# The beginning of a two-layer trunk: the first two k-tiles' scale and shift on TensorE, c loaded later, head pieces per k-tile

## The chip, the cores and the metric

The kernel runs on one core of a Trainium2 chip. The metric is device microseconds of one execution. A core has five engines that the profile names: PE (TensorE matmul, with its weight loads as PEld), DVE (VectorE), ACT (ScalarE), POOL (GpSimd) and SP (SyncE, which here issues every DMA). Each takes its instructions strictly in its own order and waits at an instruction until what that needs is there.

## The reference: what is computed

A token block `x` (256 x 2048) goes through two layers. Each layer takes `c` (1 x 2048), forms `mod = silu(c) @ w + b`, splits it into `shift`, `scale` and `gate`, and feeds the mixer with a modulated input:

```python
mod = jax.nn.silu(c) @ w + b
shift, scale, gate = jnp.split(mod, 3, axis=-1)
# every layer: x <- LayerNorm(alpha*x + (1+gate) * mixer(x*(1+scale)+shift))
```

Layer one's mixer projects `h = x*(1+scale)+shift` with `in_w` (2048 x 10304) into z, x, B, C and dt, convolves, scans and gates, and projects back. Layer two is a dilated attention. Only the first use of `mod` and the projection behind it concern the change: 2048 scales and 2048 shifts, each a dot product of length 2048, are needed before the projection can read `h`. The 2048 rows of `h` (the contraction) are 16 k-tiles of 128; k-tile kt needs its own 128 scales and 128 shifts and nothing of the other k-tiles.

## The kernel before, in words

**Columns.** For each k-tile a 1 MB "column" of `ada` (128 outputs on partitions, 2048 inputs along the free dimension) is loaded for the scale and one for the shift (`ada_load`, L242). DVE multiplies it by `cb_` (silu of c on all 128 partitions, loaded by `bcast` at L67 as 1 MB and passed through Silu at L68) and sums along the free dimension in one instruction (`ada_dot`, L251). `ada_bias` (L256) adds the bias, ACT forms `htmp = x*scale+shift` (L413) and its rounded copy `hhi` (L414), DVE the rest `hlo` (L415); both are slices of the tile that the profile calls `actT`. `h_step` (L397) does one column; two make a k-tile.

**Pieces.** Weights come in 512 KB pieces `raw` (`load_piece`, L91, six buffers). `split` (L96) makes two tiles of each: `whi` on ACT (L99) and `wlo = raw - whi` on DVE (L101), four buffers each. TensorE then multiplies hi by hi, hi by lo and lo by hi. A piece of type "cm" (B, C, x columns; `cm_piece`, L125 to L127) holds two k-tiles of 512 output columns and is 24 products of 256 columns; a "tm" piece (z; `tm_mults`, L173 to L175) is 12 products of 512 columns. Every piece is about the same PE time.

**Order of the beginning.** A list of rows (L424) fixes the order of the pieces by hand: `b4:0.` is piece 0 (k-tiles 0 and 1) of column group b4, the dot says that the partial sum is put away into SBUF by ACT (L488), and `h` is a piece of the first four column groups, alternately of `win[0]` and `win[4]`, which accumulate in PSUM through all 16 k-tiles. As k-tiles become ready one by one, TensorE works on groups that use only the ready ones. A loop (L491 on) fetches piece and column ahead, splits pieces i and i+1, multiplies piece i, and runs `h_step` so that about four columns go with seven pieces (L519). Before the loop four columns and four pieces are requested and k-tiles 0 and 1 finished. A scheduler then sets the final order on each engine; SP issues the DMAs in the order in which they are requested, with at most eight under way.

Of the kernel before, what the change touches and what calls it, by code (L numbers as in the profile page):

```python
# [18 lines left out]
P = 128  # L19
L = 256  # L20
# [29 lines left out]
def trunk(ctx, tc, xT, x, c, par, cst, bias, lnrow, ada, wdt, win, wxs, wout, wk, wv, wbin, wbout, out):  # L50
# [16 lines left out]
    bcast(cb_, c)  # L67
    S.activation(cb_, cb_, AF.Silu)  # L68
# [4 lines left out]

    cons.tile([P, 32], F32, name="pad")
# [215 lines left out]
    with ExitStack() as cA:  # L290
# [14 lines left out]
        with ExitStack() as cS:  # L305
# [4 lines left out]
            begun = {("z", 0): (win[6], 6, szt[0]), ("z", 1): (win[7], 4, szt[1]),  # L310
                     ("xs", 1): (win[5], 4, as_cm(y[0])), ("bc", 2): (win[1], 4, as_cm(y[1])),
                     ("z", 2): (win[8], 14, y[2]), ("bc", 4): (win[2], 12, as_cm(y[3])), ("z", 4): (win[10], 6, y[4]),
                     ("bc", 6): (win[3], 12, as_cm(y[5])), ("z", 6): (win[12], 10, y[6]), ("z", 5): (win[11], 8, y[7])}
# [39 lines left out]
            def product(kind, g, pre=None):  # L353

                if kind == "xs" and g > 1:
                    return xs_wide(g)

                src, k0, part = begun.get((kind, g), (None, 0, None))
                if src is None:
                    src = win[{"bc": g // 2, "xs": 4 + g, "z": 6 + g}[kind]]  # L360
                if kind == "z":
                    ps = tm_chunk(src, hh_, hl_, rate=R, k0=k0, pre=pre)
                    if g not in sz:
                        sz[g] = p0.tile([P, 2, 512], F32, name="sz")
                    for b in range(2):
                        if part is not None:
                            V.tensor_tensor(part[:, b, :], ps[b], part[:, b, :], op=ALU.add)
                        S.activation(sz[g][:, b, :], part[:, b, :] if part is not None else ps[b], AF.Silu)
                    return
                ps = cm_quad(src, hhi, hlo, rate=R, k0=k0)  # L370
                t = tiles(ps)
                if part is not None:
                    for w in range(2):
                        V.tensor_tensor(part[:, 2 * w:2 * w + 2, :], ps[w], part[:, 2 * w:2 * w + 2, :], op=ALU.add)
                    t = [part[:, n, :] for n in range(4)]
                if kind == "xs":
                    xs_conv(g, t)
                else:
                    bc_conv(g, t)

            with ExitStack() as c0:
# [4 lines left out]
                raws, xts, late = [], {}, []  # L386
# [10 lines left out]
                def h_step():  # L397
# [4 lines left out]
                    if kind == "scale" and kt % 2 == 0 and kt:  # L402
                        fetch_x(kt)
                    ada_dot(0, kind, kt, raw)
                    if kt > 1:
                        pin[0] = None
# [11 lines left out]
                h_step.i = 0  # L418
# [5 lines left out]
                for row in ("b4:0. b6:0. h z2:0. b2:0 x1:0 h", "b2:1. x1:1. z1:0 z1:1. z4:0 h h",  # L424
# [3 lines left out]
                    for w in row.split():  # L428
                        if w == two:
                            n = -2 if sum(o[0] == -2 for o in order) == sum(o[0] == -1 for o in order) else -1  # L430
                            order.append((n, sum(o[0] == n for o in order), False))
# [3 lines left out]
                source = {"dt": wdt, -2: win[0], -1: win[4], **{n: p[0] for n, p in zip(names, begun.values())}}  # L435
                pss = {-2: first[0], -1: first[1]}
# [7 lines left out]
                fetch()  # L444
                fetch()
                fetch_x(0)
                nc.sync.dma_start(adab_, par[:, :NB])
                V.tensor_scalar(adab[:, :, :, 1:3], adab[:, :, :, 1:3], 1.0, None, op0=ALU.add)
                fetch_piece()
                fetch_piece()  # L450
                fetch()
                fetch_piece()
                for _ in range(2):
                    for _ in range(2):
                        h_step()
                    while late:
                        pin[0] = late.pop()().ins
                    fetch_piece()
# [31 lines left out]
                begin, done, ended, halves = {}, set(), [], {}  # L490
                for i, (k, q, ends) in enumerate(order):  # L491
                    fetch_piece()
                    if i == 16:
                        nc.sync.dma_start(prm, par[:, NB:])
# [10 lines left out]
                    z = str(k)[0] == "z"  # L505
# [4 lines left out]
                    if z:  # L510
# [8 lines left out]
                    while h_step.i < min(len(cols), 4 + (i + 1) * 4 // 7):  # L519
                        h_step()  # L520
# [555 lines left out]
def _layout(x, c, ada_w, ada_b, ln_g, ln_b, a_in_w, a_conv_w, a_conv_b, a_dt_bias,  # L1076
# [29 lines left out]
    def mask(delta, win_, dil):  # L1106
# [6 lines left out]
    ada = ada_w.reshape(2, D, 3, KT, P).transpose(0, 2, 3, 4, 1)  # L1113
# [4 lines left out]
    win = _pieces(np.concatenate([bc, xs[:, :1024], z], 1))  # L1118
    return {
        "xT": x[0].T.reshape(KT, P, L).transpose(1, 0, 2), "x": x[0], "c": c, "par": par, "cst": cst, "bias": bias,  # L1120
        "lnrow": np.stack([ln_g[0], ln_b[0], ln_g[1], ln_b[1]]),
        "ada": ada, "wdt": _dt(dt), "win": win, "wxs": _pieces(xs[:, 1024:], 256, 4),
# [23 lines left out]
```

## Time and profile before

| what | value |
|---|---|
| median of 3 runs | 1253.88 us (1252.72 to 1255.48) |
| the profiled execution's own time | 1253.52 us |
| its span in the profile | 1251.7 us |
| mean granted TensorE clock in the span | 0.998 |
| PE busy, share of the span | 1218.4 us, 97% |
| DVE busy, ACT busy | 1031.0 us, 704.5 us |
| HBM read | 332.47 MB |

All times below count from the start of the span. Starts and durations in the timeline rows are microseconds; a bracket behind a row says how long its engine had stood idle and what ended that. The rows that the argument uses are shown with it.

### The profile page before, as it was taken

To read this page: it belongs to the slowest core of one execution; us is meant where nothing else is said; L and a number is where in the kernel's file an instruction comes from. 1 tells how busy PE (TensorE), PEld (TensorE's weight loads), DVE (VectorE), ACT (ScalarE), POOL (GpSimd) and SP (SyncE) were. 2 spreads that over 40 slices of the span, in tenths; PEclk is the share of its full clock that TensorE was granted. 3 is DMA by queue.
4 is the path that set the end of the run, shared out by engine and by line. 5 is a ranking of instruction groups with operands and counts; after the bars stand their busy time and mean duration, and the time that the engine had idled before them with its cause. 6 is when DMAs were issued, how large, how long until landed. Compare 5 with 4: busy or idle time off the path is not lost.

```text
span 1251.7 us, 18740 instructions
## 1 busy us (share of the span) xinstructions
PE 1218.4 (97%) x7086; PEld 1043.1 (83%) x7086; DVE 1031.0 (82%) x1454; ACT 704.5 (56%) x1045; POOL 0.2 (0%) x4
## 2 busy tenths in 40 slices
PE   4999999999999999999999999999999999999997
PEld 4889998898888878788888788888878888888886
DVE  6999986999987988899778678879888866758777
ACT  3655477869588788754444544434445644445631
POOL 0000000000000000000000000000000000000000
PEclk9999999999999999999999999999999999999999
DMA  9999977687657556699998569989998774464641
GB/s 381 422 421 423 420 253 257 207 286 285 203 179 219 170 155 198 220 321 342 354 313 305 183 199 377 364 318 348 359 381 317 242 241 142 126 207 122 228 176 67
DMA packets 80586, 335.88 MB, mean 268 GB/s; under 512 B 9104, under 2 KB 9328, under 8 KB 67696
## 3 DMA queue, kind: packets, MB, share of 16 engines
q1 hardware_dynamic: 80496, 334.69, 74.7%
q8 instruction: 55, 0.90, 0.3%
q14 instruction: 35, 0.29, 0.1%
HBM read 332.47 MB, written 2.18 MB: 267 GB/s over the span
## 4 chain that ended last, share of the span: by engine, by line
PE 86%; DVE 6%; DMA 5%; issue 1%; ACT 1%; SPq 0%; DVEq 0%; ACTq 0%
PE acc L149 20%; PE acc L174 12%; PE acc L175 12%; PE acc L173 12%; PE acc L152 10%; PE acc L125 4%; PE acc L127 3%; PE acc L126 3%; DMA raw<-in_wk 3%; DMA araw<-in_ada 2%; DVE araw L251 1%; DVE wlo L101 1%; PE py L625 1%; DMA raw<-in_wv 1%; PE acc L809 1%
## 5 line engine op out<-in xcount | busy, mean ns | idle before, releaser
L99 ACT ACTIVATE whi<-raw 128x1024 fp32r<-128x1024 f32 x392 | 412.3, 1058 | 383.1 <-PE acc L175 142.1
L101 DVE TENSOR_TENSOR wlo<-raw,whi 128x1024 fp32r<-128x1024 f32 x392 | 473.5, 1222 | 141.0 <-ACT whi L99 137.0
L149 PE MATMUL acc<-actT,whi 128*128 128x512 f32 x1280 | 406.3, 398 | 0.0
L152 PEld LDWEIGHTS acc<-actT,wlo 128*128 128x128 f32 x1280 | 239.7, 188 | 62.2 <-DVE wlo L101 7.2
L174 PE MATMUL acc<-wlo,actT 128*128 128x512 f32 x688 | 269.9, 392 | 0.6 <-DVE wlo L101 0.5
L173 PE MATMUL acc<-whi,actT 128*128 128x512 f32 x688 | 266.6, 394 | 1.2 <-ACT actT L681 1.2
L152 PE MATMUL acc<-actT,wlo 128*128 128x256 f32 x1280 | 254.1, 280 | 3.9 <-DVE wlo L101 3.8
L251 DVE SCALAR_TENSOR_TENSOR araw<-araw,cb__72 128x2048 f32<-128x2048 f32 x96 | 219.4, 2285 | 8.9 <-DMA araw<-in_ada 8.6
L149 PEld LDWEIGHTS acc<-actT,whi 128*128 128x128 f32 x1280 | 196.5, 189 | 0.4
L175 PE MATMUL acc<-whi,actT 128*128 128x512 f32 x432 | 168.8, 391 | 0.0
L174 PEld LDWEIGHTS acc<-wlo,actT 128*128 128x128 f32 x688 | 129.3, 188 | 28.5 <-DVE wlo L101 2.8
L173 PEld LDWEIGHTS acc<-whi,actT 128*128 128x128 f32 x688 | 128.8, 188 | 27.2 <-ACT actT L681 1.7
L125 PE MATMUL acc<-actT,whi 128*128 128x256 f32 x384 | 109.0, 288 | 17.5 <-ACT actT L414 17.3
L126 PE MATMUL acc<-actT,whi 128*128 128x256 f32 x384 | 108.8, 286 | 0.0
L127 PE MATMUL acc<-actT,wlo 128*128 128x256 f32 x384 | 106.7, 286 | 1.9 <-DVE wlo L101 1.9
L175 PE MATMUL acc<-whi,ylo 128*128 128x512 f32 x256 | 100.7, 394 | 0.0
L175 PEld LDWEIGHTS acc<-whi,actT 128*128 128x128 f32 x432 | 81.1, 188 | 16.7
L125 PEld LDWEIGHTS acc<-actT,whi 128*128 128x128 f32 x384 | 74.3, 194 | 18.9 <-ACT actT L414 17.5
L127 PEld LDWEIGHTS acc<-actT,wlo 128*128 128x128 f32 x384 | 73.4, 195 | 2.2 <-DVE wlo L101 2.1
L126 PEld LDWEIGHTS acc<-actT,whi 128*128 128x128 f32 x384 | 74.7, 194 | 0.3
L175 PEld LDWEIGHTS acc<-whi,ylo 128*128 128x128 f32 x256 | 48.1, 188 | 9.7
L583 ACT ACTIVATE seg<-cbc,cumT 128x128 f32<-128x128 f32 x128 | 41.2, 390 | 5.6 <-PE py L625 4.9
(262 smaller groups left out, 1054.3 us busy)
## 6 DMA issues: line engine op xcount, KB each, us to landing
araw<-in_ada SPq DMA_DIRECT2D x96, 1024.0 KB, 7.7
raw<-in_win SPq DMA_DIRECT2D x112, 512.0 KB, 6.5
raw<-in_wout SPq DMA_DIRECT2D x64, 512.0 KB, 5.7
raw<-in_wbin SPq DMA_DIRECT2D x64, 512.0 KB, 4.1
raw<-in_wxs SPq DMA_DIRECT2D x48, 512.0 KB, 4.6
raw<-in_wv SPq DMA_DIRECT2D x48, 512.0 KB, 6.0
raw<-in_wk SPq DMA_DIRECT2D x48, 512.0 KB, 8.3
cbc<-cumd SPq DMA_DIRECT2D x16, 512.0 KB, 4.8
```

Of the source, the lines that this page charges most:

```text
L99: copied.append(S.activation(hi, raw, AF.Copy))
L101: latest.append(V.tensor_tensor(lo, raw, hi.bitcast(F32), op=ALU.subtract))
L125: T.matmul(o, hi[:, k, c_], ahi[:, kt, :], start=first, stop=False, skip_group_check=True)
L126: T.matmul(o, hi[:, k, c_], alo[:, kt, :], start=False, stop=False, skip_group_check=True)
L127: T.matmul(o, lo[:, k, c_], ahi[:, kt, :], start=False, stop=kt == k1 - 1, skip_group_check=True)
L149: T.matmul(ps[n], hi[:, k, n * P:n * P + P], both(kt), start=kt == 0, stop=False, skip_group_check=True)
L152: T.matmul(ps[n][:, 0, :], lo[:, k, n * P:n * P + P], high(kt), start=False, stop=kt == KT - 1, skip_group_check=True)
L173: T.matmul(o, h_, hi[:, k, :], start=kt == k0, stop=False, skip_group_check=part)
L174: T.matmul(o, h_, lo[:, k, :], start=False, stop=False, skip_group_check=part)
L175: end = T.matmul(o, l_, hi[:, k, :], start=False, stop=kt == k1 - 1, skip_group_check=part)
L251: V.scalar_tensor_tensor(raw, raw, 1.0, cb_, op0=ALU.mult, op1=ALU.mult, accum_out=mod[layer][:, ct, j:j + 1])
L583: S.activation(seg[:, hh, b, :], cbc[:, hh, b, :], AF.Relu, bias=cumT[:, b, h0 + hh:h0 + hh + 1], scale=-1.0)
```

## The change

k-tiles 0 and 1 no longer use columns, `cb_` or DVE's dot. Their weights are stored by input row: four 512 KB pieces per k-tile, each 128 inputs by (four input blocks of 128 scale/shift outputs). For each piece `ada_partial` runs four small products on TensorE: a stationary `ctile` of 32 columns of which only the first holds silu(c), and 256 moving columns, each product into its own 32 partitions of one PSUM tile. Sixteen products sum a k-tile; `ada_sum` copies that tile to SBUF on ACT, two products with ones add the 128 partitions up, DVE adds the bias, and ACT and DVE form `hhi` and `hlo` directly from x. silu(c) for this comes from a new small input `cT` (128 x 16). `cb_` is loaded in two halves behind the first pieces, and its Silu is done after k-tile 1. Twelve products of a 128 x 128 tile of ones stand at the head of TensorE's queue ("warm").

The head groups (`h`) become one piece per k-tile (`whead`: 1024 output columns of one k-tile, `head_piece`), where each piece before held 512 columns of two k-tiles. The row list starts with `h h`, and one `h` of the first two rows moves. The columns begin with k-tile 2 (`h_step.i = 4`) and their pace has a slightly other formula. The rest of the program only has other indices into `win`.

```diff
+                ctile = cs[:, 0:2, :].rearrange("p i l -> p (i l)").rearrange("p (k m) -> p k m", m=32)
+                V.memset(ctile, 0.0)
+                S.activation(ctile[:, :, 0], ccol, AF.Silu)
+                def ada_rows(kt, q):
+                    return load_piece(ada[0, q // 2, kt][:, 1024 * (q % 2):1024 * (q % 2) + 1024])
+                def ada_partial(pp, q, raw):
+                    for j in range(4):
+                        T.matmul(pp[32 * j:32 * j + 32, :], ctile[:, 4 * q + j, :], raw[:, L * j:L * j + L],
+                                 start=q == 0, stop=q == 3, skip_group_check=True)
+                def ada_sum(kt, pp):
+                    part = cs[:, 2 + kt, :]
+                    S.activation(part, pp, AF.Copy)
+                    pc = mm.tile([P, 2, L], F32, name="acc")[:, 0, 0:2]
+                    for j in range(2):
+                        T.matmul(pc[:, j:j + 1], part[:, j * P:j * P + P], ones[:, 0:1], start=True, stop=True)
+                    V.tensor_tensor(mod[0][:, kt, 0:2], pc, adab[:, 0, kt, 0:2], op=ALU.add)
+                    x_, t = xts[0][:, kt, :], pe.tile([P, L], F32, name="htmp")
+                    S.activation(hhi[:, kt, :], x_, AF.Identity, bias=shift(0, kt), scale=scale(0, kt))
+                    V.tensor_scalar(t, x_, scale(0, kt), shift(0, kt), op0=ALU.mult, op1=ALU.add)
+                    return V.tensor_tensor(hlo[:, kt, :], t, hhi[:, kt, :].bitcast(F32), op=ALU.subtract)
...
-                h_step.i = 0
+                h_step.i = 4
...
-                for row in ("b4:0. b6:0. h z2:0. b2:0 x1:0 h", "b2:1. x1:1. z1:0 z1:1. z4:0 h h",
+                for row in ("h h b4:0. b6:0. z2:0. b2:0 x1:0", "h b2:1. x1:1. z1:0 z1:1. z4:0 h",
...
+                warm = mm.tile([P, 2, L], F32, name="acc")[:, 0, :P]
+                for _ in range(12):
+                    T.matmul(warm, ones, ones, start=True, stop=True)
+                rows0 = [ada_rows(0, q) for q in range(4)]
                 nc.sync.dma_start(adab_, par[:, :NB])
...
+                for q in range(4):
+                    ada_partial(pp[1], q, rows1[q])
+                    head_piece(0, halves[0], (2 * q, 2 * q + 1))
+                pin[0] = ada_sum(1, pp[1]).ins
+                for h in (slice(0, D // 2), slice(D // 2, D)):
+                    S.activation(cb_[:, h], cb_[:, h], AF.Silu)
...
-                    while h_step.i < min(len(cols), 4 + (i + 1) * 4 // 7):
+                    while h_step.i < min(len(cols), 4 + (i + (i > 7)) * 4 // 7):
```

How the beginning of SP's queue stood before (`cb__72` is `cb_`, `araw` a column, `raw` a piece, `xt` two k-tiles of x, `adab` the bias):

```order
L63 DMA cb__72<-in_c 128x2048
L244 DMA araw<-in_ada 128x2048 x2
L395 DMA xt<-in_xT 128x512
L447 DMA adab<-in_par 128x96
L93 DMA raw<-in_win 128x1024 x2
L244 DMA araw<-in_ada 128x2048
L93 DMA raw<-in_win 128x1024
L244 DMA araw<-in_ada 128x2048 x2
```

and how it stands now, up to the first two columns (`pad` holds the small cT, `raw<-in_ada` are the rows of k-tiles 0 and 1, four each, `in_whead` a head piece):

```order
L68 DMA pad<-in_cT 128x16
L91 DMA raw<-in_ada 128x1024 x4
L474 DMA adab<-in_par 128x96
L419 DMA xt<-in_xT 128x512
L91 DMA raw<-in_whead 128x1024
L91 DMA raw<-in_ada 128x1024 x4
L91 DMA raw<-in_whead 128x1024
L91 DMA raw<-in_win 128x1024 x2
L63 DMA cb__72<-in_c 128x1024 x2
L242 DMA araw<-in_ada 128x2048
L419 DMA xt<-in_xT 128x512
L91 DMA raw<-in_win 128x1024 x2
```

`cb_` moved from the first place to behind twelve pieces, and the first column from second place to behind `cb_`.

The first rows of DVE before (L251 is the dot of a column, L101 a piece's `wlo`, L256 the bias, L415 `hlo`):

```order
L251 SCALAR_TENSOR_TENSOR araw,mod_84<-araw,cb__72 128x2048 x2
L448 TENSOR_SCALAR adab<-adab 128x32x2
L256 TENSOR_TENSOR mod_84<-mod_84,adab 128x2
L101 TENSOR_TENSOR wlo<-raw,whi 128x1024
L415 TENSOR_TENSOR actT<-htmp,actT 128x256
```

and the rows of DVE now, from k-tile 1's bias (L406) to the dots of k-tile 3 (L99 is now a piece's `wlo`, L249 the dot, L254 the bias, L410 and L441 `hlo`):

```order
L406 TENSOR_TENSOR mod_83<-acc,adab 128x2
L409 TENSOR_SCALAR htmp<-xt,mod_83 128x256
L410 TENSOR_TENSOR actT<-htmp,actT 128x256
L99 TENSOR_TENSOR wlo<-raw,whi 128x1024 x3
L249 SCALAR_TENSOR_TENSOR araw,mod_83<-araw,cb__72 128x2048
L99 TENSOR_TENSOR wlo<-raw,whi 128x1024 x2
L249 SCALAR_TENSOR_TENSOR araw,mod_83<-araw,cb__72 128x2048
L254 TENSOR_TENSOR mod_83<-mod_83,adab 128x2
L99 TENSOR_TENSOR wlo<-raw,whi 128x1024
L441 TENSOR_TENSOR actT<-htmp,actT 128x256
L99 TENSOR_TENSOR wlo<-raw,whi 128x1024
L249 SCALAR_TENSOR_TENSOR araw,mod_83<-araw,cb__72 128x2048 x2
```

The four dots of k-tiles 0 and 1 are gone from the front, and the first dot now stands behind both of the new k-tiles and four `wlo`.

The first rows of PE now, with buffer numbers (L472 the products of ones, L396 the small products, L405 the sums over partitions, L500 and L502 a head piece's hi by hi and hi by lo; `raw_141` to `raw_147` are k-tile 0's rows, `raw_155` k-tile 1's first):

```order
L472 MATMUL acc_128<-ones_78 128x128 x12
L396 MATMUL acc_181<-raw_141,xs_125 32x256 x4
L396 MATMUL acc_181<-raw_143,xs_125 32x256 x4
L396 MATMUL acc_181<-raw_145,xs_125 32x256 x4
L396 MATMUL acc_181<-raw_147,xs_125 32x256 x4
L405 MATMUL acc_200<-ones_78,xs_125 128x1 x2
L500 MATMUL acc_121<-actT_87,whi_208 128x256
L502 MATMUL acc_121<-actT_87,whi_208 128x256
L500 MATMUL acc_122<-actT_87,whi_208 128x256
L502 MATMUL acc_122<-actT_87,whi_208 128x256
L500 MATMUL acc_123<-actT_87,whi_208 128x256
L396 MATMUL acc_182<-raw_155,xs_125 32x256 x4
```

Before, PE's queue began with the products of piece b4:0. Now k-tile 1's small products stand between the products of the first head piece, which already need k-tile 0. From the dt pieces (behind the last `h`) to the end of the program the instructions stand in the same order on PE, DVE, ACT and SP as before.

More of the change, by code (lines that the diff above doesn't have):

```diff
@@ L429, in trunk @@
                         if w == two:
[L430 to L431 removed]
+                            order.append((two, sum(o[0] == two for o in order), False))
                         else:
```

86 lines of the change are left out of this document (55 added, 31 removed).

## The prediction

> **What bounds the kernel now.** I read the page first (busy shares, slices, then the costliest groups), then the waits of PE over the beginning, then windows of it, and last the timeline up to 80 us.
>
> From the page, the busy line and three slice rows (each digit is a tenth of the engine in a fortieth of the span, 31.3 us):
>
> ```profile
> PE 1218.4 (97%) x7086; PEld 1043.1 (83%) x7086; DVE 1031.0 (82%) x1454; ACT 704.5 (56%) x1045; POOL 0.2 (0%) x4
> ...
> PE   4999999999999999999999999999999999999997
> ...
> DVE  6999986999987988899778678879888866758777
> ...
> DMA  9999977687657556699998569989998774464641
> ```
>
> PE is full except in the first slice and the last. The first slice is what the change works on, and whatever PE loses or gains there passes to the end, unless a later wait gives it back. The waits of PE up to 330 us show what there is to win:
>
> ```profile
> PE acc L125 <- ACT actT L414: 17.3, 2, 15.1
> PE acc L127 <- DVE wlo L101: 1.9, 1, 1.9
> PE acc L174 <- DVE wlo L101: 0.5, 1, 0.5
> ```
>
> Three waits make 19.2 us: 15.1 until k-tile 0 is there, 2.2 until k-tile 1 is (the rest of the 17.3), 1.9 for the `wlo` of b2:0. Later waits of this stretch are half a microsecond. Three windows behind them (columns: length, then busy time and count of PE, PEld, DVE, ACT, POOL, the granted clock, DMA share, GB/s):
>
> ```profile
> 25.00:50.00 25.00, 23.08 (x174) 21.82 (x174) 22.78 (x24) 15.84 (x23) 0.00 (x0) 1.00 1.02 421
> 50.00:100.00 50.00, 50.00 (x285) 44.07 (x283) 46.39 (x51) 27.42 (x37) 0.00 (x0) 1.00 1.02 421
> 100.00:150.00 50.00, 50.00 (x376) 48.11 (x375) 47.58 (x51) 25.59 (x32) 0.00 (x0) 1.00 1.02 423
> ```
>
> This is the view that matters. In the beginning three engines are nearly full at once: PE 50.00 of 50, DVE 46.39 and 47.58, the DMA engines at a share of 1.02. An earlier first product is therefore kept only if DVE's `wlo` and the landings come earlier by as much. PE is the longest of the three once it runs, so it doesn't wait again.
>
> **The front: landings.** DMA moves 421 GB/s, so a 512 KB piece (0.524 MB) takes 1.245 us and a 1 MB column 2.49. When the stream starts is read from `cb_`, whose landing releases ACT; the dot behind it has its duration beside it:
>
> ```profile
> 5.41 1.91 ACT L68 ACTIVATE cb__72<-cb__72 128x2048 f32<-128x2048 f32 x1 [3.40 <-DMA cb__72<-in_c]
> ...
> 7.98 2.29 DVE L251 SCALAR_TENSOR_TENSOR araw<-araw,cb__72 128x2048 f32<-128x2048 f32 x1 [6.98 <-DMA araw<-in_ada]
> ```
>
> 5.41 less 2.49 is 2.9, the start; the next 1 MB lands at 7.98. In the new order cT (0.3, an estimate from its 8 KB beside a landing's fixed part) and four pieces of rows land by 2.9 + 0.3 + 4 x 1.245 = 8.2. Bias and x are next. Their issues and landings before:
>
> ```profile
> L395 SPq DMA_DIRECT2D xt<-in_xT x1: 660/660/660, 2.1 to 2.1; - x1
> DMA to landing us min/median/max: 9.6/9.6/9.6
> ...
> L447 SPq DMA_DIRECT2D adab<-in_par x1: 441/441/441, 2.8 to 2.8; - x1
> DMA to landing us min/median/max: 9.5/9.5/9.5
> ```
>
> x landed at 11.7, 1.4 behind the second column (7.98 + 2.49 = 10.4), the bias at 12.3, 0.6 later. So: bias 8.8, x 10.2, first head piece 11.5, rows of k-tile 1 12.7 to 16.4, second head piece 17.6, b4 and b6 20.1, `cb_` 22.6, the first column 25.1.
>
> **k-tile 0.** Before, the chain was bias, htmp, `hhi`, first product:
>
> ```profile
> 12.77 0.16 DVE L256 TENSOR_TENSOR mod<-mod,adab 128x2 f32<-128x2 f32 x1
> 12.97 0.60 ACT L413 ACTIVATE htmp<-xt,mod 128x256 f32<-128x256 f32 x1 [5.65 <-DVE mod L256]
> 13.71 1.06 ACT L99 ACTIVATE whi<-raw 128x1024 fp32r<-128x1024 f32 x1
> 14.68 0.40 ACT L414 ACTIVATE actT<-htmp 128x256 fp32r<-128x256 f32 x1
> ...
> 15.13 0.80 PE L125 MATMUL acc<-actT,whi 128*128 128x256 f32 x2 [15.13 <-ACT actT L414]
> ```
>
> Now: last rows 8.2, four small products and their tail 1.0, copy on ACT 0.4, the sums and the bias 0.7, `hhi` 0.6: 10.9. But the head piece lands at 11.5 and needs its `whi`, 1.06: the first head product at **12.6**, 2.5 us earlier than 15.13.
>
> The trace has no small product in four column groups. The nearest are these two groups, the first of full-width products (2 of 512 columns in 1.10 us), the second of products in two 64-wide halves, 64 columns each, 32 in 1.15:
>
> ```profile
> 459.84 1.10 PE L616 MATMUL aux<-xo,cb 128*128 128x512 f32 x2
> 460.87 1.15 PE L625 MATMUL py<-xd,seg 128*64 128x64 f32 x32
> ```
>
> An L616 product, in plain fp32 like the small ones, is two records of 512 columns: 1.10 less a tail of 0.16 (a product of 256 columns lasts 0.28 and the next starts 0.12 later) is 0.94, or 0.47 for 256 columns. That is the price if the groups don't run beside each other. In the L625 row a record of 64 columns takes 0.036, so two records of 256 take 0.29 where two halves run beside each other, and 0.14 if four groups do. I take **0.14**; the bounds are 0.12 (a quarter of 0.47) and 0.47. The twelve products of ones, half as many columns at about half pace, are 12 x 0.42 = 5.0 and end by 6 us, in time in which PE waited anyway: neither gain nor loss of their own but by the clock (next part); without that cover they would cost these 5.
>
> **The clock.** The products of before show two paces in their starts, 0.21 apart and then 0.12, with the change at 20.8:
>
> ```profile
> 20.21 0.41 PE L127 MATMUL acc<-actT,wlo 128*128 128x256 f32 x1
> 20.42 0.41 PE L125 MATMUL acc<-actT,whi 128*128 128x256 f32 x1
> ...
> 20.95 0.28 PE L125 MATMUL acc<-actT,whi 128*128 128x256 f32 x1
> ```
>
> PE had been busy since 15.13, so the full pace came 5.7 us after the start. Later in the kernel there is one dip of the granted clock, in three windows:
>
> ```profile
> 464.50:467.94 3.44, 1.36 (x9) 0.95 (x9) 3.42 (x5) 3.42 (x3) 0.00 (x0) 1.00 0.65 213
> 467.94:471.36 3.42, 3.42 (x12) 2.94 (x12) 3.18 (x6) 3.38 (x8) 0.00 (x0) 0.50 0.72 164
> 471.36:474.80 3.44, 3.44 (x21) 3.00 (x21) 3.36 (x5) 2.61 (x6) 0.00 (x0) 1.00 0.92 291
> ```
>
> After a window in which PE was busy 1.36 of 3.44 us, the clock was half for 3.42. In the changed kernel PE has only two tiny products between 9.2 and 12.6. I expect the same dip from about 12 to 18.8, because the window in which PE takes up again is only partly busy and the one behind it must first be full.
>
> **k-tile 1 and the dots.** From 12.6 PE has 24 head products and 16 small ones before the sums. At half clock, 24 x 0.214 and 16 x 0.28 = 9.6 us, of which the last part (from 18.8) goes at full pace: done at **21.1**. At full clock 24 x 0.12 + 16 x 0.14 = 5.1, with a tail 18.0. Then ACT does copy, `hhi`, and the `whi` of the second head piece: 2.8 to 3.0 us, in which PE waits about 2.2 (the wait at k-tile 1 of before is not removed, it changes its cause). ACT goes on with two `whi` (0.97 apart) and the two halves of `cb_`'s Silu (half of 1.91 each): 23.9 + 1.9 + 2.0 = **27.8** is when the dots may start at half clock; at full clock that is 24.9 and the column's landing at 25.1 decides.
>
> From there DVE is the longest chain. The rows of one stretch of before give its steps:
>
> ```profile
> 28.84 2.28 DVE L251 SCALAR_TENSOR_TENSOR araw<-araw,cb__72 128x2048 f32<-128x2048 f32 x1
> 31.05 0.08 DVE L251 DVE_READ_ACCUMULATOR araw<-araw,cb__72 128x1 f32 x1
> 31.17 0.16 DVE L256 TENSOR_TENSOR mod<-mod,adab 128x2 f32<-128x2 f32 x1
> 31.25 2.29 DVE L251 SCALAR_TENSOR_TENSOR araw<-araw,cb__72 128x2048 f32<-128x2048 f32 x1
> 33.46 3.49 DVE L101 TENSOR_TENSOR wlo<-raw,whi 128x1024 fp32r<-128x1024 f32 x3
> 36.87 0.42 DVE L415 TENSOR_TENSOR actT<-htmp,actT 128x256 fp32r<-128x256 f32 x1
> ```
>
> The place where it meets PE is piece z4:2, the sixteenth in both orders (fifteen pieces stand ahead of it before and now). PE began z4:1 at 62.68:
>
> ```profile
> 62.68 0.40 PE L173 MATMUL acc<-whi,actT 128*128 128x512 f32 x1
> ...
> 76.31 0.28 PE L125 MATMUL acc<-actT,whi 128*128 128x256 f32 x1
> ```
>
> Sixty such products fill the 13.63 us between the rows, 0.227 each; twelve of z4:1 and one more put the first product with the `wlo` of z4:2 at 65.6. Up to that `wlo` DVE has, from the first dot on, 9 dots of 2.28 (20.5), 4 biases of 0.11 (0.4), 12 `wlo` of 1.16 (13.9) and 4 `hlo` of 0.35 (1.4): 36.2 us. Beside that it stands idle for `whi`, `hhi` and landings: 2.5 us if it starts at 27.8, 3.8 if at 25.1 (an earlier start waits longer for columns at 30.9, 35.8 and 38.8); in 36 us of the windows above DVE was idle 1.7 to 3.2. So at half clock the `wlo` is there at 27.8 + 36.2 + 2.5 + 0.1 = 66.6, **1.0 later** than PE wanted it; at full clock at 25.1 + 36.2 + 3.8 + 0.1 = 65.2, **0.4 earlier**.
>
> PE itself gets to b2:1 up to 4.4 us earlier than before and gives it back in waits at b2:1 (1.4 to 2.8), x1:1 (0.9) and z4:2 (0.3). Behind z4:2 all three queues run as before, so 1.0 stays to the end. DVE's four dots (9.1 us) were removed from a time in which it had little else; that is why they don't count.
>
> Sum: 1253.52 (the profiled execution: span 1251.7 and 1.8 around it; the median of the runs is 0.36 above) + 1.0 = **1254.5**.
>
> **The rivals.**
>
> *The clock stays granted* through 9.2 to 12.6. For: between 22.26 and 24.76 of before PE stood 2.2 us and the pace held. Against: the three windows above. It gives 1253.52 - 0.4 = 1253.1. The Trainium skill ("TensorE: Matmul & The Clock Gate", Part 1) makes this its rule: the clock falls after a whole idle window of about 3.4 us; by that 1253.1 would be the time, yet here 1.36 busy of 3.44 was followed by half clock, so I go by the row. Its window length agrees with the 3.42 of the dip.
>
> *The column groups don't run beside each other.* This is the slower one. At 0.47 a product k-tile 0 has its sums at 14.6 instead of 9.8 (sixteen products, 7.5 us, behind the products of ones and their tail), and the first head product comes at 17.0. PE then needs 24 x 0.12 + 16 x 0.47 = 10.4, with copies and tail the first product of k-tile 1 comes at 30.6, the dots at 34.5, and the `wlo` of z4:2 at 73.3: 7.7 later, 1261.2; with the half clock about 2 more, 1263. Two at a time at half clock give 2.9, 1256.4. At full clock it decides from about 0.22 per product on. For: no row has four groups. Against: the L625 row. The skill's page just named (Part 3) gives 2.38 for three groups side by side; an estimate from it for four, 0.47 / 3.2, is 0.15, and the sum would be about the same.
>
> *DVE's idle time closes.* Then the lead of PE is kept: all of it 4.2, 1249.3; half of it 1251.3. For: ACT has much room (27.42 of 50), and 100 to 150 us show DVE at 47.58. Against: in every window of the beginning DVE left some time, with the same two engines alternating.
>
> **How the numbers follow.** Forecast 1254.5, chance 0.38, its own range 1253.7 to 1257.6 (its upper end has two groups at a time and a clock that comes back later); clock granted 0.18; groups one by one 0.20 (1256.4 to 1263); idle time closed 0.22 (1249.3 to 1251.3); 0.02 others. A measurement of this kernel can tell about 0.2%, 2.5 us. Faster by more: the last rival, 0.22. Slower by more: 0.20, and 0.10 from the forecast's upper end and the rest. Within: 0.48. The range 1250.0 to 1260.5 leaves out about a tenth on each side.
>
> **What would show it.** First head product at 12.6 and its starts 0.21 apart (0.12: first rival); small products 0.14 apart at full pace; first dot at 27.8; PE waits for `wlo` at b2:1, x1:1 and z4:2, that of z4:2 at 66.6. No wait at z4:2, with PE there before 64, would make the forecast wrong, and so would small products over 0.22.

## The result and the profile after

The changed kernel takes **1257.09 us** (median of 8 runs, 1256.07 to 1258.49), the kernel before in the same runs 1253.53 (1251.90 to 1255.51). The ratio is 1.0031, 95% interval 1.0022 to 1.0040: slower by 3.6 us. The forecast was 1254.5 in a range of 1250.0 to 1260.5. The profiled execution is the slowest of the eight, 1258.49 with a span of 1256.7.

The busy line and the three slice rows of the page of the changed kernel:

```profile
PE 1231.5 (98%) x7182; PEld 1050.9 (84%) x7182; DVE 1024.5 (82%) x1449; ACT 703.7 (56%) x1047; POOL 0.2 (0%) x4
...
PE   7999999999999999999999999999999999999997
...
DVE  3999986999987988899778578888888866758777
...
DMA  9999976687656446689989569989998764464641
```

PE's first slice went from 4 to 7, DVE's from 6 to 3: the work did move from DVE to PE. PE is busy 13 us longer and the kernel isn't faster, so a fuller PE row says nothing here. The waits of PE up to 330 us (what it waited for, us in total, times, longest):

```profile
PE acc L500 <- ACT whi L97: 4.2, 2, 2.3
PE aux L651 <- DVE cb L630: 1.3, 1, 1.3
...
PE acc L125 <- DVE wlo L99: 1.2, 2, 0.6
...
PE acc L405 <- ACT xs L402: 1.0, 2, 0.5
PE acc L172 <- DVE wlo L99: 0.6, 2, 0.5
```

Of the 19.2 us of three waits the 15.1 for k-tile 0 are gone, and shorter ones stand in their place, the longest 2.3; the wait for k-tile 1 is still there (1.83 in the second row below, 2.2 before). Where the time went is seen from single places of PE's timeline: first head product, first of k-tile 1, first with the `wlo` of z4:2:

```profile
13.88 0.47 PE L500 MATMUL acc<-actT,whi 128*128 128x256 f32 x1 [2.33 <-ACT whi L97]
...
24.29 0.58 PE L500 MATMUL acc<-actT,whi 128*128 128x256 f32 x1 [1.83 <-ACT whi L97]
...
67.66 0.50 PE L172 MATMUL acc<-wlo,actT 128*128 128x512 f32 x1
```

The last was at 65.6 before: 2.0 later. One more place serves for all runs below, since it stands behind the dt pieces, where all orders are the same again: the put-away of the last z piece on DVE, first in the kernel before and then in the changed one:

```profile
186.31 1.37 DVE L486 TENSOR_TENSOR s<-acc,s 128x512 f32<-128x512 f32 x2
```

```profile
188.85 1.37 DVE L538 TENSOR_TENSOR s<-acc,s 128x512 f32<-128x512 f32 x2
```

2.5 us later. The spans of these two profiles differ by 5.0 (the medians by 3.6), and the beginning made 2.5 of it. Some of the rest is a wait of ACT for a landing at 210 (before 0.53):

```profile
210.51 1.58 ACT L640 ACTIVATE seg<-cbc,cumT 128x128 f32<-128x128 f32 x5 [1.41 <-DMA cbc<-cumd]
```

and this profiled execution lost 2 us more where DVE waited for a column, which the profile of before doesn't show; its time is 1.4 above the median:

```profile
544.20 2.29 DVE L249 SCALAR_TENSOR_TENSOR araw<-araw,cb__72 128x2048 f32<-128x2048 f32 x1 [2.17 <-DMA araw<-in_ada]
```

What lies behind the put-away varies from profile to profile: from there to the end the profiles of the runs below took from 1.4 us less (e3) to 2.5 more (the changed kernel) than that of before, so the put-away gives an execution's time only roughly.

What comes early shows where the 2.5 arose. Windows of 10 us of the kernel before (the last column is GB/s):

```profile
0.00:10.00 10.00, 0.00 (x0) 0.00 (x0) 2.20 (x3) 3.19 (x2) 0.20 (x4) 1.00 0.83 326
10.00:20.00 10.00, 4.72 (x20) 4.38 (x21) 8.02 (x12) 3.97 (x5) 0.00 (x0) 1.00 0.99 388
20.00:30.00 10.00, 7.78 (x58) 7.45 (x58) 8.42 (x9) 4.03 (x7) 0.00 (x0) 1.00 1.01 424
```

and of the changed kernel:

```profile
0.00:10.00 10.00, 7.69 (x52) 5.87 (x56) 0.70 (x4) 1.51 (x2) 0.20 (x4) 1.00 0.77 262
10.00:20.00 10.00, 7.17 (x55) 4.91 (x51) 2.38 (x5) 2.04 (x3) 0.00 (x0) 0.83 0.99 373
20.00:30.00 10.00, 7.66 (x56) 6.57 (x49) 6.43 (x7) 5.72 (x7) 0.00 (x0) 0.83 1.02 386
```

By 30 us the kernel before had moved 3.26 + 3.88 + 4.24 = 11.38 MB, the changed one 10.21. The 1.17 MB between them are 2.8 us at 422 GB/s, about what the place at 186 shows. Note the DMA share from 10 us on: 0.99 and 1.01 before, 0.99 and 1.02 after. The share doesn't tell a stream at 373 GB/s from one at 424. Two stretches of SP's queue belong to it. In the first, 2.50 to 4.50 us, the changed kernel moves 225 GB/s:

```profile
2.50:4.50 2.00, 2.00 (x11) 2.00 (x11) 0.00 (x0) 1.40 (x2) 0.00 (x0) 1.00 0.88 225
```

where before moved 410:

```profile
2.50:4.50 2.00, 0.00 (x0) 0.00 (x0) 0.00 (x0) 0.00 (x0) 0.00 (x0) 1.00 1.01 410
```

In the second SP stands, from the second head piece to b4, because no raw buffer is free: first it waits for a landing of k-tile 1's rows, and the last 2.2 us, to 16.2, for the first small products of k-tile 1 on PE. `cb_` and the first column are queued behind it:

```profile
10.50 0.33 SPq L91 DMA_DIRECT2D raw<-in_whead  x1
16.28 0.80 SPq L91 DMA_DIRECT2D raw<-in_win  x2
17.14 1.94 SPq L63 DMA_DIRECT2D cb__72<-in_c  x2
19.12 0.48 SPq L242 DMA_DIRECT2D araw<-in_ada  x1
```

Behind this stand the stream is slower: from 15 to 25 us the changed kernel moved 353 GB/s, before 426.

### The profile page after: what moved, and what is told of

It reads as the page before. It is cut to its first block, busy times and chain, and to the rows that moved or that the text cites. A ratio compares the mean times of both kernels' runs of the same rounds, so it can differ in the third digit from the quotient of the medians.

```text
span 1256.7 us, 18952 instructions
## 1 busy us (share of the span) xinstructions
PE 1231.5 (98%) x7182; PEld 1050.9 (84%) x7182; DVE 1024.5 (82%) x1449; ACT 703.7 (56%) x1047; POOL 0.2 (0%) x4
## 4 chain that ended last, share of the span: by engine, by line
PE 78%; DMA 10%; DVE 6%; ACT 3%; issue 2%; SPq 0%; DVEq 0%; ACTq 0%
PE acc L147 21%; PE acc L172 11%; PE acc L173 11%; PE acc L171 11%; PE acc L150 10%; DMA araw<-in_ada 4%; DMA raw<-in_win 2%; DVE wlo L99 2%; DVE araw L249 2%; PE acc L123 2%; PE acc L124 2%; PE acc L125 2%; DMA raw<-in_wk 1%; PE py L682 1%; ACT whi L97 1%
## 5 line engine op out<-in xcount | busy, mean ns | idle before, releaser
L99 DVE TENSOR_TENSOR wlo<-raw,whi 128x1024 fp32r<-128x1024 f32 x392 | 473.7, 1223 | 141.8 <-ACT whi L97 134.9
L150 PEld LDWEIGHTS acc<-actT,wlo 128*128 128x128 f32 x1280 | 239.8, 189 | 61.8 <-DVE wlo L99 6.6
L150 PE MATMUL acc<-actT,wlo 128*128 128x256 f32 x1280 | 253.9, 280 | 3.8 <-DVE wlo L99 3.5
L249 DVE SCALAR_TENSOR_TENSOR araw<-araw,cb__72 128x2048 f32<-128x2048 f32 x92 | 210.3, 2287 | 5.6 <-DMA araw<-in_ada 4.8
L147 PEld LDWEIGHTS acc<-actT,whi 128*128 128x128 f32 x1280 | 196.4, 189 | 0.4
L125 PE MATMUL acc<-actT,wlo 128*128 128x256 f32 x256 | 71.3, 284 | 1.2 <-DVE wlo L99 1.2
L123 PE MATMUL acc<-actT,whi 128*128 128x256 f32 x256 | 72.2, 284 | 0.0
L124 PE MATMUL acc<-actT,whi 128*128 128x256 f32 x256 | 72.0, 283 | 0.0
L125 PEld LDWEIGHTS acc<-actT,wlo 128*128 128x128 f32 x256 | 48.5, 192 | 1.6 <-DVE wlo L99 1.6
L123 PEld LDWEIGHTS acc<-actT,whi 128*128 128x128 f32 x256 | 49.0, 192 | 0.4
L124 PEld LDWEIGHTS acc<-actT,whi 128*128 128x128 f32 x256 | 49.1, 192 | 0.1
```

What stands on the lines that cost most here:

```text
L99: latest.append(V.tensor_tensor(lo, raw, hi.bitcast(F32), op=ALU.subtract))
L123: T.matmul(o, hi[:, k, c_], ahi[:, kt, :], start=first, stop=False, skip_group_check=True)
L124: T.matmul(o, hi[:, k, c_], alo[:, kt, :], start=False, stop=False, skip_group_check=True)
L125: T.matmul(o, lo[:, k, c_], ahi[:, kt, :], start=False, stop=kt == k1 - 1, skip_group_check=True)
L147: T.matmul(ps[n], hi[:, k, n * P:n * P + P], both(kt), start=kt == 0, stop=False, skip_group_check=True)
L150: T.matmul(ps[n][:, 0, :], lo[:, k, n * P:n * P + P], high(kt), start=False, stop=kt == KT - 1, skip_group_check=True)
```

## The experiments

Three theories stood against each other. **A**: TensorE's own path with its half-clock time makes the loss (the forecast's cause). **B**: DVE's chain from the first dot makes it. **C**, put forward after e4: the stream of transfers makes it; after e9, the front of the stream alone. The table has, for each run, the MB moved by 30 us, the start of the put-away that is at 186.31 in the profile of before, and the time with its ratio to the kernel before in the same job (that had 1253.5 to 1253.7).

| run | MB by 30 us | put-away at | median us | ratio, 95% interval |
|---|---|---|---|---|
| before | 11.38 | 186.31 | 1253.53 | |
| changed kernel | 10.21 | 188.85 | 1257.09 | 1.0031 (1.0022 to 1.0040) |
| e1 no warm-up | 10.13 | 189.17 | 1257.12 | 1.0032 (1.0019 to 1.0044) |
| e2 fill | 10.15 | 189.77 | 1257.59 | 1.0035 (1.0024 to 1.0047) |
| e3 early c | 10.93 | 188.11 | 1257.08 | 1.0028 (1.0017 to 1.0038) |
| e4 fill, early c | 10.79 | 188.65 | 1255.27 | 1.0014 (1.0005 to 1.0023) |
| e5 wide | 11.09 | 186.84 | 1254.46 | 1.0008 (0.9998 to 1.0018) |
| e6 wide, fill, early c | 11.07 | 187.37 | 1255.63 | 1.0012 (1.0000 to 1.0024) |
| e7 one group | 9.91 | 189.36 | 1257.09 | 1.0030 (1.0018 to 1.0043) |
| e8 before, warm-up | 11.39 | 187.25 | 1256.08 | 1.0017 (1.0009 to 1.0026) |
| e9 before, extra loads late | 11.33 | 187.75 | 1254.40 | 0.9999 (0.9990 to 1.0008) |
| e10 wide, cT second | 11.30 | 186.28 | 1254.12 | 1.0008 (0.9997 to 1.0019) |
| e11 e10 with fill | 11.26 | 186.19 | 1254.90 | 1.0012 (1.0003 to 1.0021) |
| e12 before, extra loads first | 10.18 | 192.81 | 1259.08 | 1.0039 (1.0025 to 1.0054) |

**e1, without the warm-up products.**

```diff
-                for _ in range(12):
+                for _ in range(1):
                     T.matmul(warm, ones, ones, start=True, stop=True)
```

> One product of ones at the head of TensorE's queue instead of twelve, nothing else. Theory A (TensorE's own path with its clock sets the loss): the clock is half until PE has been busy for a full window, from about 13.9 on, so the head products and k-tile 1's small products run at 0.21 and 0.28 up to 20.8; the sums of k-tile 1 come at about 23.5 instead of 21.9 and everything behind them 1.5 later: about 1258.6. Theory B (DVE's chain from the first dot decides, and the first dot waits for its column anyway): within 0.5 of the changed kernel's 1257.1. That the products of ones are a pure cost would give less than 1256.6.

1257.12: no change, though in the profile k-tile 1's first product came 1.0 later (25.29). That goes with B or C: the warm-up products neither cost nor gain.

**e2, products of ones in PE's two waits.**

```diff
                 halves[0] = split(pieces[0])
+                for _ in range(9):
+                    T.matmul(both[0][:, 1, :P], ones, ones, start=True, stop=True, skip_group_check=True)
...
                 pin[0] = ada_sum(1, pp[1]).ins
+                for _ in range(8):
+                    T.matmul(both[1][:, 1, :P], ones, ones, start=True, stop=True, skip_group_check=True)
```

> Nine products of ones behind k-tile 0's sums and eight behind k-tile 1's, in stretches in which PE waits, so that no window is mostly idle. Theory A: both half-clock stretches go (1.6 us and 1.5 us of PE), 1254.0 to 1255.5. Theory B: PE runs ahead and gives it back in waits for wlo, since the first dot still waits for a column that landed at about 27.7: 1256.3 to 1257.1. If the granted clock falls in spite of the products, the rule read from the windows (a window with PE busy about half is enough for a fall) is wrong.

1257.59, no gain, a little above B's range. In its profile no dip follows the wait for k-tile 1 any more, but the first dip stayed and came sooner (11.6 to 15.0):

```profile
7.80:11.20 3.40, 1.64 (x23) 0.64 (x19) 0.20 (x1) 0.38 (x1) 0.00 (x0) 1.00 1.02 388
11.20:14.60 3.40, 3.40 (x19) 3.40 (x19) 1.75 (x4) 1.66 (x2) 0.00 (x0) 0.56 0.99 387
```

The products of ones themselves now ran at half clock and put the first head product at 14.95 (13.88 in the changed kernel), so e2 takes away only one of the two dips. What PE gained it gave back at b2:1, where it now waited 2.29 us for `wlo` (0.61 in the changed kernel); the clock was then half again, behind that wait.

**e3 and e4, `cb_` and the first column ahead of b4 and b6,** alone and with e2's edit.

```diff
                 fetch_piece()
-                fetch_piece()
-                fetch_piece()
                 for h in (slice(0, D // 2), slice(D // 2, D)):
                     bcast(cb_[:, h], c, h.start)
                 fetch()
+                fetch_piece()
+                fetch_piece()
```

> cb_ and the first column are requested ahead of the pieces b4 and b6, nothing else in the code; the first dot can start at about 26.2 instead of 28.07 and now stands behind one wlo. Theory B: the wlo of z4:2 comes about 1.9 earlier and so does the end: 1255.2 to 1255.6. Theory A: PE can save no more than its three short waits for wlo (0.6, 0.6 and 0.2): 1255.7 to 1257.1, likeliest 1256.5.

> Both of the edits before. If PE's own path and DVE's chain lie within a microsecond of each other (A and B both hold, each for its share), the two gains add up to more than either alone: 1252.5 to 1254.0, no slower than the kernel before. Theory A alone: as e2. Theory B alone: as e3.

e3: SP still stands, from 12.9 to 16.2, but `cb_` and the first column are now ahead of the stand; the stream is 1.7 us nearer to that of before, the first dot starts at 26.38 instead of 28.07, and the median is the same. It misses B, lies at the upper end of A's range, and speaks against C too, if the bytes by 30 us were all that counts. Its second dot starts at 34.56, as in the changed kernel (34.69): between the two dots DVE waits 1.34 us for a `whi` that stands on ACT behind b4's put-away, and that waits for PE, so the gain of 1.7 is spent within one column. e4 with 1255.27 is 1.8 better, at about the same bytes by 30 us as e3, and in its profile PE kept the full clock through the whole beginning; yet the put-away is still 2.3 behind that of before. 1255.27 lies in the ranges that A alone and B alone gave, not in that of both. The two rows of b4's put-away, in e3 and in e4, show where the clock counts:

```profile
31.85 0.60 ACT L540 ACTIVATE s<-acc 128x512 f32<-128x512 f32 x1 [1.40 <-PE acc L125]
```

```profile
30.88 0.60 ACT L545 ACTIVATE s<-acc 128x512 f32<-128x512 f32 x1 [0.22 <-PE acc L125]
```

With the full clock b4 is done sooner, ACT waits 0.22 instead of 1.40, and the second dot starts at 33.60 instead of 34.56. In time the intervals of e3 and e4 overlap.

**e5, the rows of k-tiles 0 and 1 as 1 MB transfers with 8 KB per partition,** in column buffers instead of raw ones. All other code is the changed kernel's.

```diff
-                def ada_rows(kt, q):
-                    return load_piece(ada[0, q // 2, kt][:, 1024 * (q % 2):1024 * (q % 2) + 1024])
+                def ada_rows(kt):
+                    for j in range(2):
+                        raws.append(ada_load((wp1, pe)[kt], 0, KIND[j], kt))
+                    return [raws[2 * kt + q // 2][:, 1024 * (q % 2):1024 * (q % 2) + 1024] for q in range(4)]
```

> The rows of k-tiles 0 and 1 are loaded as two 1 MB transfers per k-tile with 8 KB per partition, into the buffers of the columns, so that they hold no raw buffer and SP doesn't stand at one; the products are the same. Theory C (the stream of transfers sets the pace of the first 155 us; the changed kernel's was 2.7 to 2.9 us behind that of before from the 10th MB on, 1.45 of it lost in the first 7 us, the rest between 15 and 27 us): the lag falls under 1.2 us and the time by 1.5 to 2, to 1255.0 to 1255.8. Theory A (TensorE's own path with its clock): only the first head product comes earlier, by about 1.2; 1255.8 to 1256.5. If it is neither, the time stays at 1257.

1254.46: 2.6 us better, more than C's forecast. The windows of its profile:

```profile
0.00:10.00 10.00, 7.65 (x56) 6.05 (x56) 0.85 (x4) 1.68 (x3) 0.20 (x4) 1.00 0.78 287
10.00:20.00 10.00, 7.43 (x60) 5.51 (x60) 2.22 (x4) 2.05 (x4) 0.00 (x0) 0.83 1.02 406
20.00:30.00 10.00, 8.30 (x53) 8.02 (x54) 7.72 (x9) 7.15 (x9) 0.00 (x0) 0.83 1.02 416
```

The clock column reads 0.83 twice, as in the changed kernel: both dips are still there. The stream alone is better (11.09 MB), and with it k-tile 1's first product is at 21.75 instead of 24.29.

**e6, e10 and e11** build on e5: e6 adds both edits of e4, e10 puts cT behind the first 1 MB of rows, e11 is e10 with the fill.

```diff
+                        if first and j == 0:
+                            nc.sync.dma_start(ccol, cT)
+                            S.activation(ctile[:, :, 0], ccol, AF.Silu)
```

> e5 with the edits of e2 (products of ones in PE's two waits) and of e3 (cb_ and the first column ahead of b4 and b6). Theory C with A: stream and clock both mended, the stream within 0.5 us of that of before: 1251.5 to 1253.5, as fast as the kernel before or a little faster. If only the stream counts, the same as e5 within 0.7. If DVE's chain from the first dot decides (B), about 1 below e4: 1254.2.

> e5 with the small cT requested second, behind the first 1 MB of rows, so that the stream starts with a large transfer as it did before. Theory C: the lag to before falls from 0.6 to about 0 and the time by 0.3 to 0.6 to 1253.9 to 1254.2. Theory A: the small products wait for silu(c) until about 7, which the second half of the rows hides: no change, 1254.5.

> e10 with the products of ones of e2 in PE's two waits (b4 and b6 stay ahead of cb_, unlike in e6). With the stream as early as in the kernel before, what is left is PE's half-clock time (1.5 to 3 us): if that now counts, 1251.5 to 1253.0, faster than the kernel before; if the stream alone counts, as e10; if DVE's chain does, 1254.

e6 is not better than e5 and misses all three of its forecasts: b4, put behind `cb_`, lands late and PE waits 1.5 us for its `whi`. e10 and e11 bring the stream to within 0.3 us of that of before, and the put-away to within 0.1 of 186.31, with the half clock (e10) or with less of it (e11). No version beats the kernel before; 0.9997 to 1.0019 for e10 can't be told from no change, and e10 can't be told from e5 either.

**e7, all small products in one column group.** The sums over partitions then take 32 partitions.

```diff
-                        T.matmul(pp[32 * j:32 * j + 32, :], ctile[:, 4 * q + j, :], raw[:, L * j:L * j + L],
-                                 start=q == 0, stop=q == 3, skip_group_check=True)
+                        T.matmul(pp[0:32, :], ctile[:, 4 * q + j, :], raw[:, L * j:L * j + L],
+                                 start=q + j == 0, stop=q + j == 6, skip_group_check=True)
```

> The changed kernel with its small products all in the first column group (into the same 32 partitions, summed there; the sums over partitions then take 32 partitions), so that none can run beside another. If the four groups ran beside each other in the changed kernel (0.14 to 0.16 a product), each now takes 0.43 to 0.47: k-tile 0's sums come 3 to 4 us later, k-tile 1's sixteen products take about 5 more on PE, and the time is 1263 to 1266. If they did not, it stays at 1257. As a rival of the prediction, the price of no overlap was 7.7.

The price is as expected, the time isn't. k-tile 0's sixteen products (32 records) in e7:

```profile
6.43 7.07 PE L396 MATMUL acc<-raw,xs 128*32 128x256 f32 x32 [0.32 <-DMA raw<-in_ada]
```

are 0.44 each; eight of e5 in four groups

```profile
8.69 1.07 PE L398 MATMUL acc<-araw,xs 128*32 128x256 f32 x16 [1.07 <-DMA araw<-in_ada]
```

are 0.134 each, so the four groups run beside each other, 3.3 times as fast. k-tile 1's sums come at 26.1 instead of 21.9, but the first dot only at 29.46 instead of 28.07 and the first `wlo` product of z4:2 at 68.47 instead of 67.66, and the median is 1257.09 to the digit. PE had that much room: its clock stayed full throughout in this profile, and the scheduler put k-tile 0's part of b4 into the wait for k-tile 1 (an order that the edit also changed). A rival of the prediction, with 7.7 us for it, would have been wrong even if its condition had held.

**e8, the kernel before with 46 warm-up products.**

```diff
+                warm = mm.tile([P, 2, L], F32, name="acc")[:, 0, :P]
+                for _ in range(46):
+                    T.matmul(warm, ones, ones, start=True, stop=True)
                 fetch()
                 fetch()
                 fetch_x(0)
```

> The kernel before with 46 products of ones at the head of TensorE's queue, which end just ahead of k-tile 0 at 15.1, and nothing else of the change. Theory A: the products of b4:0 and b6:0 run at the full clock from the start, 2.4 us less, of which PE keeps all if nothing else is late: 1251.1. Rival: k-tile 1 comes at 24.8 in any case (DVE's dots and the columns' landings), PE only waits longer there, and the time stays within 0.5 of 1253.5; the longer wait (4.7 us) could then even halve the clock behind it and cost 1.5: 1255.

The rival's mechanism holds, but the time is longer than it gave: with the products of b4:0 and b6:0 at full pace, k-tile 1 still comes at 25.67, and PE waits 1.62 for `whi` and 2.49 for k-tile 1 instead of 2.22. The median is 2.4 us worse, with the bytes by 30 us as before (11.39 MB): the stream's front is not the only thing that can cost 2 us here. The profiled execution is the fastest of the twelve and has only 0.9 of it at the put-away. That the longer waits halve the clock in the others is a guess; no profile here shows it, and the cause stays open.

**e9 and e12, the kernel before with three unread loads of the tile cc,** late in SP's queue (27 to 46 us) and in its front (8 to 25 us). Nothing else is changed.

```diff
+                    if i in (2, 4, 6):
+                        nc.sync.dma_start(cc, cst)
```

```diff
                 fetch()
                 fetch_piece()
+                for _ in range(3):
+                    nc.sync.dma_start(cc, cst)
```

> The kernel before with three extra loads of the constant tile cc (328 KB each, 0.98 MB in all, 2.3 us of the stream at 421 GB/s) in SP's queue ahead of the seventh piece of the loop; nothing reads them, and the products, the clock and DVE's work are those of before. Theory C (stream): PE comes later by most of the 2.3, less what the stream had in hand: 1255.0 to 1256.0. Theory A or B (an engine's own path sets the pace and the stream only keeps up): within 0.5 of 1253.7.

> As e9, the kernel before with three unread loads of cc (0.98 MB, 2.3 us of the stream), but in the front of SP's queue: one ahead of the fourth column, one ahead of the fifth, one behind it, so that the stream is late from about 15 us on instead of from about 35 us. If the stream sets the pace only at the front (what the changed kernel lost there, e5 won back, and e9's later delay didn't cost), k-tile 1 comes 0.8 later and the pieces and columns behind it up to 2.3: 1254.8 to 1256.0. If an engine's own path sets the pace at the front as well: as e9, within 0.7 of 1253.6.

e9: no change (0.9990 to 1.0008, so at most 1.0 us), and C is wrong as first stated: behind about 30 us the stream had at least 1.3 of the 2.3 us in hand. (Its profiled execution is 1.4 late at the put-away and shows a clock of 0.83 in the window 30 to 40, where before shows 1.00.) e12: 1259.08, 5.3 slower, more than expected, since each load of cc waits for the one before and SP stands meanwhile:

```profile
10.32 0.33 SPq L244 DMA_DIRECT2D araw<-in_ada  x1
19.24 0.33 SPq L454 DMA_DIRECT2D cc<-in_cst  x1
19.66 0.38 SPq L244 DMA_DIRECT2D araw<-in_ada  x1
24.83 0.33 SPq L454 DMA_DIRECT2D cc<-in_cst  x1
```

It had moved 10.18 MB by 30 us, two to three loads of 0.33 of them unread: 1.9 to 2.2 MB or 4.4 to 5.2 us behind, and 5.3 is what it lost (3.1 to 6.8 by the interval). In e9 SP stood as long for the loads of cc (11.4 us, here 12.1), and no loss could be measured. So in the kernel before a late front costs about all of its lateness, and lateness 20 us on costs little or nothing. That the front makes the changed kernel's loss rests on e5, which mends little else and wins 2.6, and on e10, which can't be told from the kernel before; e3, e4 and e8 show that the bytes are not the whole account.

**One place joins the three theories: the second dot.** It starts at 34.69 in the changed kernel, 35.63 in e1, 34.56 in e3, 33.60 in e4, 32.81 in e5, 33.80 in e6, 35.50 in e7, 32.52 in e10 and 32.15 in e11. The row of the changed kernel:

```profile
34.69 2.28 DVE L249 SCALAR_TENSOR_TENSOR araw<-araw,cb__72 128x2048 f32<-128x2048 f32 x1
```

In each of these nine profiles PE uses the first `wlo` of z4:2 33.0 us later (32.96 to 33.00), and its weight load waits 0.3 us for it; only e2 differs there. So from the second dot to z4:2 DVE's chain sets the pace, which is the path that the forecast named. B took it from the first dot, and there it isn't tight yet. What starts the chain is what comes ahead of the second dot: in the changed kernel DVE waits 1.26 and 0.69 us for `whi`, the first behind a landing at 30.5, and in e3 PE's half clock has its part. e11, whose z4:2 comes 0.5 earlier than in the kernel before (65.11 for 65.65), is no faster than that, so an earlier start than that is not kept; what takes it back was not followed.

## Why the prediction was right and where it failed

**Right: slower by little.** The forecast went the right way, the range held the time, and the size was off: +1.0 by its own sum, +2.0 at its own place (z4:2), +2.5 behind the dt pieces, 3.6 by the medians. That the range held is luck in part, since most of the loss came from a term that the sum had too small, the landings.

**Landings: the step that failed.** "DMA moves 421 GB/s", and the new order's landings were added up from that. The rate of a saturated stretch was used for a front that had another shape: 225 GB/s in 2.5 to 4.5 us with 4 KB per partition where before had 410 with 8 KB, and a queue that stands. The prediction named the buffers nowhere in its sum, though eight rows in six raw buffers can't be requested ahead of PE. Its 0.3 for cT came from no row; e10, which asks for cT second, had moved 0.15 MB more than e5 by 10 us, 0.36 us at 421 GB/s, so that term was about right. k-tile 0's last rows, reckoned for 8.2, reached PE at 9.80. ACT's rows show the further misses:

```profile
12.77 1.06 ACT L97 ACTIVATE whi<-raw 128x1024 fp32r<-128x1024 f32 x1 [0.39 <-DMA raw<-in_whead]
...
30.54 1.06 ACT L97 ACTIVATE whi<-raw 128x1024 fp32r<-128x1024 f32 x1 [2.50 <-DMA raw<-in_win]
```

The first head piece was reckoned for 11.5 and landed at 12.77; hence the first head product at 13.88 and not 12.6. The fifth piece landed at 30.5, and its `whi` is what DVE waits for ahead of the second dot. e5 mends the landings alone and wins 2.6 of the 3.6.

**Small products at 0.14: right** (0.134 in four groups). My full price, 0.47, was 0.44. The twelve products of ones were reckoned too short, 5.0 in place of 5.6 by the same 0.47; they took 5.49, to 6.54, and e1 shows that this cost nothing.

**The clock: the mechanism was right, its weight wrong.** I expected one dip from about 12 to 18.8. There were two, each a window of 3.4 us:

```profile
7.21:10.62 3.41, 1.97 (x28) 0.47 (x24) 0.20 (x1) 0.11 (x1) 0.00 (x0) 1.00 1.03 385
10.62:14.04 3.42, 0.76 (x5) 0.68 (x6) 1.18 (x4) 1.93 (x3) 0.00 (x0) 1.00 1.01 396
14.04:17.45 3.41, 3.41 (x19) 2.38 (x20) 1.05 (x1) 0.00 (x0) 0.00 (x0) 0.50 0.97 393
...
20.87:24.28 3.41, 1.09 (x12) 0.52 (x4) 1.00 (x4) 1.97 (x4) 0.00 (x0) 1.00 0.98 335
24.28:27.69 3.41, 3.40 (x16) 3.40 (x17) 3.41 (x3) 3.41 (x4) 0.00 (x0) 0.50 1.01 417
```

PE busy 0.76 and 1.09 of 3.41 was followed by half clock, 1.97 of 3.41 was not. Yet in e2 the window ahead of the dip, 8.22 to 11.63, had PE busy 2.02 of 3.41, so the busy share alone does not give the rule; it stays open. The dips did not make most of the loss: e5 has both and is 2.6 faster; e4 has neither, and its put-away is as late as the changed kernel's but for 0.2, though its median is 1.8 better. In this stretch, in which PE waits for landings, its pace counted only where another engine waited for it, as ACT does in e3.

**k-tile 1 and the dots: the chain right, its start partly by accident.** The first dot was forecast for 27.8 and came at 28.07, released by `cb_`'s Silu as forecast; the later landing and the shorter dip nearly cancel in it. The waits at b2:1 (0.6), x1:1 (0.6) and z4:2 (0.2) are where they were named, the first two smaller than named (1.4 to 2.8 and 0.9). DVE's idle time up to z4:2, reckoned 2.5, came to 3.2 and was most of the miss. I laid it to DVE alternating with ACT; 1.95 of it lies between the first and the second dot, and 1.26 of that goes back to the piece that landed at 30.5. The chain from there to z4:2, and the place where it meets PE, were right.

**"All three queues run as before, so 1.0 stays to the end"** held only nearly: 2.0 at z4:2 became 2.5 at 186, and the wait for cbc at 210 added up to 0.9 in this profile (PE's wait there was at most 1.3 us in the runs of the table). Why that landing varies stays open.

**The rivals.** The clock that stays granted didn't come about, and what the Trainium skill ("TensorE: Matmul & The Clock Gate", Part 1) says, that the clock falls after a whole idle window, is not what these windows show (PE busy 0.76 and 1.09 of 3.41); the length of a window agrees. DVE's idle time didn't close. That the stream itself would come late was in none of the cases, and a rival of that kind ("the rows land later than the columns did, and everything in the front with them", 1.2 MB, 2.8 us, 1256.3) was the one to have.

## What to carry to other kernels

In a front where every landing is used at once, count the bytes moved by a fixed time, before and after, and divide the difference by the rate: that gave 2.8 us here of a 2.5 us loss, where busy shares of engines and of DMA gave nothing. It is a first count and not a proof: e3 won back 1.7 us of the bytes and no time, and e8 lost 2.4 us with none behind. When a change gives rows or pieces to other buffers, follow the queue that issues the loads: a load that waits for a buffer holds all that are queued behind it. Look for the engine whose rows keep the same distances in every version (here DVE from the second dot on) and ask what releases the first of them. And ask of an engine's pace (a warm clock, fewer products) whether it is waited for in that stretch; keeping it busy is no gain by itself.

## What was not expected of the hardware

The DMA engines were busy for a share of 0.88 at 225 GB/s at the start with 4 KB per partition, and 1.01 at 410 GB/s with 8 KB; in the same two microseconds e5, with 8 KB and cT in front, moved 299, and e10, with cT second, 381. So the size of the rows is not all of it; packet size, cT's place and the number of loads under way were not told apart further. In the changed kernel the two dips of the clock begin at 14.04 and 24.28, 3 x 3.41 apart; in e2 the first begins at 11.6, with the same products in the same order up to 11.35, so these products do not set where a dip begins. The column of the granted clock does not show every half pace: before reads 1.00 from 10 to 20 us, where its products start 0.21 apart. The executions of one kernel spread over 2 to 6 us (the changed kernel 1256.07 to 1258.49, e10 1251.64 to 1257.68, the kernel before 1251.47 to 1256.31 in its longest series), which is as much as most of the edits here are worth; why is not shown.
